# The first layer's down product and the short convolution's output product with tokens on partitions, in a two-layer decoder trunk

## The chip, the cores and the metric

The kernel runs on one core of a Trainium2 chip. The metric is the device time of one execution in microseconds. Before the change three runs took 2530.51 to 2531.64 us, with a median of 2531.28 us.

## The reference

Input and output are 256 tokens of 2048 features in float32. Layer 0 has a Mamba-2 mixer, layer 1 a short gated convolution; a gated feed-forward with a convolution over tokens follows each. Cut to what matters here:

```python
def rms_norm(x, w):
    y = x * rsqrt(mean(x * x, axis=-1) + 1e-5)
    return y * w

def conv_ffn(u, w_up, conv_w, conv_b, w_down):        # w_up 2048 x 11264, w_down 5632 x 2048
    hu = causal_dwconv(u @ w_up, conv_w, conv_b)       # width 3, over tokens
    g, v = split(hu, 2, axis=-1)
    return (silu(g) * v) @ w_down

def short_conv_mixer(u, w_in, conv_w, w_out):          # w_in 2048 x 6144, w_out 2048 x 2048
    bg, cg, h = split(u @ w_in, 3, axis=-1)
    return (bg * causal_dwconv(cg * h, conv_w)) @ w_out

x = x + ssd_mixer(rms_norm(x, mix_norm_w[0]), ...)
x = x + conv_ffn(rms_norm(x, ffn_norm_w[0]), ...)      # layer 0
x = x + short_conv_mixer(rms_norm(x, mix_norm_w[1]), ...)
x = x + conv_ffn(rms_norm(x, ffn_norm_w[1]), ...)      # layer 1
return rms_norm(x, final_norm_w)
```

## The kernel before

Every product is taken as three products of a split operand: a float32 array is cast to a high part in a reduced float32 format (`fp32r`), and the low part is what is left. High by high, high by low and low by high are added up in PSUM; low by low is left out.

**Weights.** All weights are loaded in blocks of 256 rows by 512 columns (`KU` = 2 tiles of 128 rows, `COLS` = 512), 512 KB each, in the order of the list `plan`, into four buffers `raw` (`load_raw`, line 330). `recipes` says what is made of them. A plain unit is one block's high part `wh` (ScalarE, line 352) and low part `wl` (VectorE, line 353). The units sit in four buffers and are made up to three ahead of use; `weight_unit` hands out the next. The program is written in order, and a scheduler places each engine's instructions by a simulated timeline; matmuls that go through `follow` keep their written order on TensorE.

**Streaming form** (`stream`, `late_stream`; features on partitions). The weights are the stationary operand, 128 by 128, and the activations of all 256 tokens the moving one. An activation tile `hl` has the high parts of 256 tokens and then the low parts, so `wh` takes one matmul of 512 columns and `wl` one of 256 (line 466). A unit is 8 of each. The result of four feature tiles lies in two PSUM tiles of two banks. `late_stream` works the second pair of feature tiles one unit behind the first; its argument `settle` sets how many matmuls of `wh` go before those of `wl`. All of the residual `x` lies in eight tiles `xp` with features on partitions. `residual_stream` adds a product to them (lines 854 and 855), squares them for the norm (`Norm.add`) and splits the next operand (`split_pair`). `Norm.row` sums the squares over partitions by matmuls (`tok_sum`, line 236), takes the reciprocal root per token, and spreads it over partitions by two matmuls (`bcast_tok`, line 229). The factor is applied to the next product's result, so the next product need not wait for it.

**Token form** (`down_tok`, line 1034; tokens on partitions). The activations are stationary, 128 tokens by 128 features, and the weights move, 512 columns at a time (lines 1070 to 1072: high by `wh`, high by `wl`, low by `wh`). So a block against both halves of the tokens is 2 x 2 x 3 = 12 matmuls. The residual lies in two tiles `xtok` of 128 tokens by 2048 features, and PSUM results are added to it by `add_x` (line 1080). The output columns go in two halves of two column groups. In a half the pairs of row blocks are worked in the order of a tuple in `DOWN`: a plain number is a pair of blocks (one for each column group), worked by 24 matmuls; `~j` is pair `j` worked by seven products in place of eight (Strassen's scheme in Winograd's form over two token halves, two row tiles and two column groups), 21 matmuls. For these `token_sums` makes sums and differences of the activations, and `load_unit` makes sums and differences of two weight blocks that are held together: recipes `t12`, `raw`, `t34` and `b22` (lines 374 to 383, on VectorE with casts on ScalarE). After a half's last such pair their seven sums are put together and added (the entry `e`).

Before the change the token form is used in layer 1's down product alone. Layer 1's feed-forward begins with the turn of `xp` into `xtok` by 32 transposes (line 997). The feed-forwards work their 5632 hidden features in two parts (`FPARTS`): part 0 has 24 tiles of 128 rows, part 1 has 20; each part's up product is followed by its down product. Stages in order: Mamba mixer (to about 704 us), layer 0's up and down products in two parts, the short convolution's input and output products, and layer 1's feed-forward, which ends with the final norm on `xtok`.

PSUM has three tiles of two banks (`psm`, tag `main`) and two of one bank (`psa`, tag `aux`).

Of the kernel before, what the change touches and what calls it, by code (L numbers as in the profile page):

```python
# [16 lines left out]
P = 128  # L17
# [31 lines left out]
def trunk_kernel(ctx, tc, a, out):  # L49
# [174 lines left out]
    def bcast_tok(r, dg=None):  # L224

        dg = dg or diag_tok(r)
        ps = aux()
        for c in range(2):
            mm(ps[:, c * P : (c + 1) * P], ones, dg[:, c, :], start=True, stop=True)
        return ps[:, :T]  # L230
# [87 lines left out]
    planned_all(c_out, 0, NKD)  # L318
# [124 lines left out]
    def late_stream(c0, hls, kcs, evac, settle=None):  # L443
# [395 lines left out]
    def residual_stream(hls, kcs, norm, nhl, nname, put=stream, parts=ALL_COLS):  # L839
# [7 lines left out]
        for cg, lo, hi in parts:  # L847
# [14 lines left out]
            put(cg * COLS, hls[lo // 2 : hi // 2], kcs[lo:hi], evac)  # L862
# [37 lines left out]
    def token_sums(y):  # L900


        st = pair_tmp()
        h0, h1 = slice(0, P), slice(P, T)
        tt(out=st[:, 0, h0], in0=y[:, 0, h1], in1=y[:, 1, h1], op=ALU.add)
        tt(out=st[:, 0, h1], in0=st[:, 0, h0], in1=y[:, 0, h0], op=ALU.subtract)
        tt(out=st[:, 1, h0], in0=y[:, 0, h0], in1=y[:, 0, h1], op=ALU.subtract)
        tt(out=st[:, 1, h1], in0=y[:, 1, h0], in1=st[:, 0, h1], op=ALU.subtract)
        sh, sl = (xpool.tile([P, 2, T], F32R, tag="x", name=uid("x")) for _ in range(2))
        nc.scalar.copy(sh, st)  # L910
        tt(out=sl, in0=st, in1=sh.bitcast(F32), op=ALU.subtract)
        return [(q[:, n // 2, (n % 2) * P : (n % 2 + 1) * P]) for n in range(4) for q in (sh, sl)]

    def ffn_part(l, part, hls, r):
        lo, hi = FPARTS[part]
        res, sums = [], {}
        for ch in range(lo, hi, 4):
            gs = []

            def evac_g(p, pt, ch=ch):  # L920
                k0 = ch + 2 * p
                y = conv(scaled(pt, r), W_FF, f"fw{l}", NF, k0, f"fb{l}", "g", gpool)
                act(y, y, AF.Silu)
                gs.append(y)

            def evac_v(p, pt, ch=ch):
                k0 = DFF // P + ch + 2 * p
                y = conv(scaled(pt, r), W_FF, f"fw{l}", NF, k0, f"fb{l}")
                tt(out=y, in0=gs[p], in1=y, op=ALU.mult)
                h = new_hl(hlpool2 if len(res) < 4 else hlpool)  # L930
                split_pair(h, y)
                if l == 1 and ~len(res) in DOWN[part][0] + DOWN[part][1]:
                    sums[len(res)] = token_sums(y)
                res.append(h)

            settle = {(0, 0): (2, None), (1, 0): (1, 1), (1, 4): (1, None), (1, 24): (2, 1)}
            settle = settle.get((l, ch), (None, None))
            late_stream(ch * P, hls, range(NKD), evac_g, settle[0])
            late_stream(DFF + ch * P, hls, range(NKD), evac_v, settle[1])
        return res, sums  # L940

    xhl, nhl = nhl, []
    r = norm.row()
    norm = Norm()
    for part in range(2):
# [8 lines left out]
    xhl, nhl = nhl, []  # L954
    r = norm.row()
    norm = Norm()
    r2 = small.tile([P, T], F32, tag="r2", name="r2", bufs=1)
    tt(out=r2, in0=r, in1=r, op=ALU.mult)
    yhl = []
    settle = {(0, 1): 1, (0, 2): 1}  # L960
    for i in range(D // COLS):
        vs = [None, None]

        def evac_c(p, pt):
            s = pair_sum(pt)
            tt(out=s, in0=s, in1=rep2(r2), op=ALU.mult)
            vs[p] = s

        def evac_h(p, pt):
            s = pair_sum(pt)  # L970
            tt(out=s, in0=s, in1=vs[p], op=ALU.mult)
            vs[p] = conv(s, W_SC, "scw", NKD, 4 * i + 2 * p)

        def evac_b(p, pt):
            s = scaled(pt, r)
            tt(out=s, in0=s, in1=vs[p], op=ALU.mult)
            h = new_hl()
            split_pair(h, s)
            yhl.append(h)

        for n, ev in ((1, evac_c), (2, evac_h), (0, evac_b)):
            late_stream(n * D + i * COLS, xhl, range(NKD), ev, settle.get((i, n)))
    residual_stream(
        yhl, range(NKD), norm, nhl, lambda m: ("ffn", NKD + 2 * m), late_stream
    )


    xhl = nhl
    r = norm.row()
# [13 lines left out]
    ss = small.tile([P, 2, 4], F32, tag="ss", name=uid("ss"))  # L1003

    most = [None, None]

    def begin_mean(c):

        sst = small.tile([P, 1], F32, tag="sst", name=uid("sst"))
        nc.vector.tensor_reduce(out=sst, in_=ss[:, c, 0:3], op=ALU.add, axis=mybir.AxisListType.X)  # L1010
        most[c] = small.tile([P, 1], F32, tag="most", name=uid("most"))
        ts(out=most[c], in0=sst, scalar1=0.5 / D, scalar2=0.5 * EPS, op0=ALU.mult, op1=ALU.add)

    def finish(c):

        v = small.tile([P, 1], F32, tag="var1", name=uid("var1"))
        stt(out=v, in0=ss[:, c, 3:4], scalar=0.5 / D, in1=most[c], op0=ALU.mult, op1=ALU.add)
        r = rsqrt_half(v)
        for q in (0, 1, 3, 2):
            x = xtok[c][:, q * COLS : (q + 1) * COLS]  # L1020
            if q == 3:
                stt(out=x, in0=x, scalar=r[:, 0:1], in1=fin[:, 3 * COLS :], op0=ALU.mult, op1=ALU.mult)
            elif q == 0:
                ts(out=x, in0=x, scalar1=r, scalar2=None, op0=ALU.mult)
            else:
                act(x, x, AF.Copy, scale=r)
            (nc.sync if q in (0, 3) else nc.scalar).dma_start(
                out=out[0, c * P : (c + 1) * P, q * COLS : (q + 1) * COLS], in_=x
            )

# [3 lines left out]
    def down_tok(hid, sums, lo, halves, done):  # L1034
# [7 lines left out]

        for half, order in enumerate(halves):
            cgs = (2 * half, 2 * half + 1)
            m23, m15, m67 = main_pair(), main_pair(), main_pair()
            bank = {
                1: m15[:, 0, :], 5: m15[:, 1, :], 6: m67[:, 0, :], 7: m67[:, 1, :],
                2: m23[:, 0, :], 3: m23[:, 1, :], 4: aux(), 8: aux(),
            }
            tail = order is LAST and half == 1  # L1050
            work = []
            for at, j in enumerate(order):
# [4 lines left out]
                elif not (tail and at >= len(order) - 2):  # L1057
                    work += [("p", j, m) for m in (2, 4, 3, 8)]
# [24 lines left out]
            for i, (kind, j, m) in enumerate(work):  # L1083
                if kind == "p":
# [5 lines left out]
                    if tail and i == len(work) - 5:  # L1090
# [3 lines left out]
                        block_done_of(done, 0, cgs[1])  # L1094
                elif kind == "s":
                    if m in (5, 1, 7, 3):
# [7 lines left out]
                else:  # L1104
                    add_x(0, 0, bank[1])
                    u = [tmp.tile([P, 512], F32, tag="tp", name=uid("tp")) for _ in range(3)]
# [13 lines left out]
            for m, c, g in () if tail else ends:  # L1120
                block_done_of(done, c, cgs[g])
    def block_done_of(done, c, cg):
        if done is not None:
            done(c, cg)

    for part in range(2):
        lo, hi = FPARTS[part]
        hid, sums = ffn_part(1, part, xhl, r)
# [44 lines left out]
```

## Time and profile before

| | before |
|---|---|
| median of three runs | 2531.28 us |
| the profiled execution's own time | 2532.64 us |
| span of its trace | 2530.8 us |
| granted TensorE clock, mean | 0.998 |
| HBM read | 474.09 MB |
| streaming matmuls of the late stages, line 466 | 4544 and 4544 |
| weight blocks of the down products, loaded | 176 x 512 KB |
| weight blocks of the short convolution's output product | 32 x 512 KB |

PE is the matmul engine, PEld its weight loads, DVE is VectorE, ACT ScalarE, POOL GpSimd and SP the engine that issues the weight loads. The chain is followed back from the last instruction: at each step to what released it, or to the instruction before it on its engine. In rows of the timeline the first number is the start in us from the span's beginning, the second the duration; in brackets stands an idle time before it with what ended it. Matmuls overlap, so the pace is the distance between starts and not the duration. A row of the waits says who waited for whom: the time in total, how often, and the longest.

### The profile page before, as it was taken

To read this page: it belongs to the slowest core of one execution; us is meant where nothing else is said; L and a number is where in the kernel's file an instruction comes from. 1 tells how busy PE (TensorE), PEld (TensorE's weight loads), DVE (VectorE), ACT (ScalarE), POOL (GpSimd) and SP (SyncE) were. 2 spreads that over 40 slices of the span, in tenths; PEclk is the share of its full clock that TensorE was granted. 3 is DMA by queue.
4 is the path that set the end of the run, shared out by engine and by line. 5 is a ranking of instruction groups with operands and counts; after the bars stand their busy time and mean duration, and the time that the engine had idled before them with its cause. 6 is when DMAs were issued, how large, how long until landed. Compare 5 with 4: busy or idle time off the path is not lost.

```text
span 2530.8 us, 37056 instructions
## 1 busy us (share of the span) xinstructions
PE 2510.2 (99%) x14358; PEld 2187.7 (86%) x14358; DVE 1868.8 (74%) x2630; ACT 1383.3 (55%) x1801; POOL 1.1 (0%) x8
## 2 busy tenths in 40 slices
PE   9999999999999999999999999999999999999998
PEld 8888888888888888888888888888888887888887
DVE  7788875788777776557776666666677778778787
ACT  5676654566555554345554444444555555455554
POOL 0000000000000000000000000000000000000000
PEclk9999999999999999999999999999999999999999
DMA  7566655665666665566666666665666666666654
GB/s 235 173 190 198 188 179 187 198 176 173 200 183 191 189 189 190 191 191 190 189 189 190 191 185 191 191 192 188 178 186 190 191 188 195 199 189 189 190 196 161
DMA packets 255731, 478.67 MB, mean 189 GB/s; under 512 B 17667, under 2 KB 29123, under 8 KB 255427
## 3 DMA queue, kind: packets, MB, share of 16 engines
q1 hardware_dynamic: 254643, 474.13, 61.8%
q8 instruction: 112, 1.84, 0.3%
q10 hardware_dynamic: 912, 2.18, 0.2%
q14 instruction: 64, 0.52, 0.1%
HBM read 474.09 MB, written 2.16 MB: 188 GB/s over the span
## 4 chain that ended last, share of the span: by engine, by line
PE 94%; DVE 3%; DMA 2%; ACT 0%; issue 0%; SPq 0%; DVEq 0%; ACTq 0%
PE main L466 62%; PE main L429 16%; PE main L412 8%; PE main L1071 1%; PE main L1072 1%; PE main L1070 1%; DMA raw<-in_ffn_w_down_dram 1%; DVE wl L353 1%; PE aux L1071 1%; PE aux L1070 1%; PE aux L1072 1%; PE aux L797 1%; DVE wl L383 1%; DMA cbc<-cs_d 0%; PE aux L805 0%
## 5 line engine op out<-in xcount | busy, mean ns | idle before, releaser
L466 PE MATMUL main<-hl,wh 128*128 128x512 f32 x4544 | 1568.4, 391 | 0.0
L353 DVE TENSOR_TENSOR wl<-raw,wh 128x1024 fp32r<-128x1024 f32 (+1 forms) x868 | 1058.7, 1222 | 583.0 <-ACT wh L352 573.7
L352 ACT CAST wh<-raw 128x1024 fp32r<-128x1024 f32 (+1 forms) x868 | 910.7, 1050 | 945.7 <-PE main L466 614.7
L466 PE MATMUL main<-hl,wl 128*128 128x256 f32 x4544 | 1256.0, 280 | 0.0
L466 PEld LDWEIGHTS main<-hl,wh 128*128 128x128 f32 x4544 | 845.1, 187 | 180.8
L466 PEld LDWEIGHTS main<-hl,wl 128*128 128x128 f32 x4544 | 856.4, 189 | 6.2
L429 PE MATMUL main<-hl,wh 128*128 128x512 f32 x1728 | 542.4, 397 | 1.3 <-DVE tp L492 1.3
L412 PEld LDWEIGHTS main<-hl,wl 128*128 128x128 f32 x1792 | 332.1, 188 | 75.6 <-DVE wl L353 2.8
L412 PE MATMUL main<-hl,wl 128*128 128x256 f32 x1792 | 359.8, 281 | 1.6 <-DVE wl L353 1.6
L429 PEld LDWEIGHTS main<-hl,wh 128*128 128x128 f32 x1728 | 266.5, 189 | 7.8 <-issue 4.9
L484 ACT COPY tp<-main 128x512 f32<-128x512 f32 x150 | 87.2, 581 | 30.9 <-PE main L466 23.9
L486 DVE TENSOR_TENSOR tp<-main,tp 128x512 f32<-128x512 f32 x150 | 102.4, 683 | 1.4 <-ACT tp L484 1.4
L508 DVE SCALAR_TENSOR_TENSOR tp<-tp,prm,tp 128x255 f32<-128x255 f32 x208 | 88.5, 477 | 0.0
L495 DVE TENSOR_TENSOR tp<-tp,rrow 128x512 f32<-128x512 f32 x118 | 81.3, 689 | 2.5
L508 DVE SCALAR_TENSOR_TENSOR g<-tp,prm,g 128x254 f32<-128x254 f32 (+1 forms) x176 | 73.4, 478 | 1.2 <-ACT g L506 1.2
L1071 PE MATMUL main<-wl,hl 128*128 128x512 f32 x150 | 58.4, 390 | 0.0
L1072 PE MATMUL main<-wh,hl 128*128 128x512 f32 x150 | 58.4, 389 | 0.0
L1070 PE MATMUL main<-wh,hl 128*128 128x512 f32 x150 | 58.4, 389 | 0.0
L382 ACT CAST wh<-tp 128x512 fp32r<-128x512 f32 x52 | 30.3, 617 | 43.2 <-DVE tp L374 40.5
L1071 PE MATMUL aux<-wl,hl 128*128 128x512 f32 x137 | 53.3, 389 | 0.0
L1072 PE MATMUL aux<-wh,hl 128*128 128x512 f32 x137 | 53.3, 389 | 0.0
L1070 PE MATMUL aux<-wh,hl 128*128 128x512 f32 x137 | 53.3, 389 | 0.0
(177 smaller groups left out, 1440.7 us busy)
## 6 DMA issues: line engine op xcount, KB each, us to landing
raw<-in_ffn_w_up_dram SPq DMA_DIRECT2D x352, 512.0 KB, 3.7
raw<-in_ffn_w_down_dram SPq DMA_DIRECT2D x176, 512.0 KB, 4.2
raw<-in_ssd_w_in_dram SPq DMA_DIRECT2D x159, 512.0 KB, 4.7
raw<-in_sc_w_in_dram SPq DMA_DIRECT2D x96, 512.0 KB, 3.7
raw<-in_ssd_w_out_dram SPq DMA_DIRECT2D x64, 512.0 KB, 3.8
raw<-in_sc_w_out_dram SPq DMA_DIRECT2D x32, 512.0 KB, 3.6
cbc<-cs_d SPq DMA_DIRECT2D x32, 256.0 KB, 6.0
xt<-in_x_dram SPq DMA_DIRECT2D x8, 256.0 KB, 6.8
```

The source lines that it names most:

```text
L352: put(nc.scalar.copy(wh[:, ks, :], raw[:, ks, :]))
L353: put(tt(out=wl[:, ks, :], in0=raw[:, ks, :], in1=wh[:, ks, :].bitcast(F32), op=ALU.subtract,))
L412: put(mm(pts[t // 2][:, t % 2, 0:T], wl[:, k, t * P : (t + 1) * P], hls[i // 2][:, i % 2, 0:T], start=False, stop=(i == n - 1),))
L429: put(mm(o, wh[:, k, lw], hl, start=first, stop=False))
L466: follow(mm(pts[p][:, t % 2, cols], w[:, k, t * P : (t + 1) * P], hl[:, cols], start=(i == 0 and w is wh), stop=(i == n - 1 and w is wl),))
L484: nc.scalar.copy(pb, pt[:, :, T : 2 * T])
L486: tt(out=s, in0=pt[:, :, 0:T], in1=pb, op=ALU.add)
L495: tt(out=s, in0=s, in1=rep2(r), op=ALU.mult)
L508: stt(out=y[:, j, d:T], in0=s[:, j, 0 : T - d], scalar=pcol(wname, (width - 1 - d) * nk + k0 + j), in1=y[:, j, d:T], op0=ALU.mult, op1=ALU ...
L1070: follow(mm(bank[m], ah, wh[:, k, :], start=first, stop=False))
L1071: follow(mm(bank[m], ah, wl[:, k, :], start=False, stop=False))
L1072: follow(mm(bank[m], al, wh[:, k, :], start=False, stop=last))
```

## The change

Layer 0's down product (both parts) and the short convolution's output product are worked by `down_tok`. The residual is turned into `xtok` once, ahead of layer 0's feed-forward, and stays with tokens on partitions from there on. What the next product needs with features on partitions is turned back: eight groups `turn(m)` of four transposes into one PSUM bank, from which `split_pair` makes an operand tile. The first four groups are put into the second half of the down product (entries `t`), the other four between the first units of the next product (`then`). The sum of squares is taken per token by ScalarE's accumulator (`TokNorm.add`), so the sum over partitions goes; the spreading over partitions stays. In a half with turns the banks are given out in another way (`apart`), so that `aux` tiles are free for the transposes. The order of layer 1's part 0 changes too: `~6` and `~9` each stand one place later.

```diff
 DOWN = (
-    ((1, 2, ~0, 4, 5, ~3, 7, ~6, 8, ~9, 10, 11), (1, 2, ~0, 4, 5, ~3, 7, ~6, 8, ~9, 10, 11)),
+    ((1, 2, ~0, 4, 5, ~3, 7, 8, ~6, 10, ~9, 11), (1, 2, ~0, 4, 5, ~3, 7, 8, ~6, 10, ~9, 11)),
     ((1, 2, ~0, 4, 5, ~3, 7, ~6, 8, 9), (1, 2, ~0, 4, 5, ~3, 6, 7, 8, 9)),
 )
+DOWN_TURN = (DOWN[0], (DOWN[1][0], (1, 2, 4, 5, ~0, 6, 7, ~3, 8, 9)))
+SC_TURN = ((1, 2, 0, 4, ~3, 5, 6, 7), (1, 2, 0, 4, 5, ~3, 6, 7))
...
-            if l == 1:
-                planned_tok(a["ffn_w_down"][l], lo, DOWN[part])
-            else:
-                planned_all(a["ffn_w_down"][l], lo, hi)
+            planned_tok(a["ffn_w_down"][l], lo, (DOWN if l else DOWN_TURN)[part])
...
-    planned_all(c_out, 0, NKD)
+    planned_tok(c_out, 0, SC_TURN)
...
-    def late_stream(c0, hls, kcs, evac, settle=None):
+    def late_stream(c0, hls, kcs, evac, settle=None, then={}):
...
             if u:
                 half(1, u - KU)
+            for f in then.get(u // KU, ()):
+                f()
...
+    class TokNorm:
+        def add(self, c, cg):
+            junk = tmp.tile([P, 512], F32, tag="tp", name=uid("tp"))
+            x = xtok[c][:, cg * COLS : (cg + 1) * COLS]
+            act(junk, x, AF.Square, accum_out=self.ss[:, c, cg : cg + 1])
+
+        def turn(self, m):
+            ps = aux()
+            for j in range(2):
+                for c in range(2):
+                    k = 2 * m + j
+                    follow(nc.tensor.transpose(
+                        ps[:, j * T + c * P : j * T + (c + 1) * P],
+                        xtok[c][:, k * P : (k + 1) * P], ident,
+                    ))
+            h = new_hl()
+            split_pair(h, ps.rearrange("p (a b) -> p a b", b=T), *self.nname(m))
+            self.nhl[m] = h
...
+        def then(self, pend, *more):
+            return {
+                1: pend[:1], 2: [pend[1], self.chain], 3: pend[2:3], 4: pend[3:],
+                6: [self.row, *more],
+            }
...
+    def down_tok(hid, sums, lo, halves, done=None, turn=None):
+        pend = []
         for half, order in enumerate(halves):
             cgs = (2 * half, 2 * half + 1)
-            m23, m15, m67 = main_pair(), main_pair(), main_pair()
-            bank = {
-                1: m15[:, 0, :], 5: m15[:, 1, :], 6: m67[:, 0, :], 7: m67[:, 1, :],
-                2: m23[:, 0, :], 3: m23[:, 1, :], 4: aux(), 8: aux(),
-            }
+            apart = turn is not None and half == 1
+            m23 = main_pair()
+            bank = {2: m23[:, 0, :], 3: m23[:, 1, :]}
+            if apart:
+                m48 = main_pair()
+                bank[4], bank[8] = m48[:, 0, :], m48[:, 1, :]
+            else:
+                bank[4], bank[8] = aux(), aux()
+            def more_banks():        # called at the half's first pair by seven products
+                m15 = main_pair()
+                bank[1], bank[5] = m15[:, 0, :], m15[:, 1, :]
+                if apart:
+                    bank[6], bank[7] = aux(), aux()
+                else:
+                    m67 = main_pair()
+                    bank[6], bank[7] = m67[:, 0, :], m67[:, 1, :]
...
                 elif not (tail and at >= len(order) - 2):
-                    work += [("p", j, m) for m in (2, 4, 3, 8)]
+                    for m in (2, 4, 3, 8):
+                        work.append(("p", j, m))
+                        if apart and (at, m) in ((0, 8), (1, 4), (1, 8), (2, 8)):
+                            work.append(("t", None, None))
...
+                elif kind == "t":
+                    pend.pop(0)()
...
+            elif turn is not None:
+                ends = ((4, 1, 0), (2, 0, 0), (8, 1, 1), (3, 0, 1))
...
+            if turn is not None:
+                pend += [(lambda m=m: turn(m)) for m in range(4 * half, 4 * half + 4)]
+        return pend
...
-                if l == 1 and ~len(res) in DOWN[part][0] + DOWN[part][1]:
+                if ~len(res) in DOWN[part][0] + DOWN[part][1]:
                     sums[len(res)] = token_sums(y)
...
-            settle = {(0, 0): (2, None), (1, 0): (1, 1), (1, 4): (1, None), (1, 24): (2, 1)}
+            settle = {
+                (0, 0): (1, 1), (0, 4): (1, None), (0, 24): (2, 1),
+                (1, 0): (2, 1), (1, 4): (1, None), (1, 24): (2, 1),
+            }.get((l, ch), (None, None))
...
-        hid, _ = ffn_part(0, part, xhl, r)
-        last = part == 1
-        residual_stream(
-            hid, range(*FPARTS[part]), norm if last else None, nhl,
-            lambda m: ("mix", NKD + 2 * m), late_stream,
-        )
+        hid, sums = ffn_part(0, part, xhl, r)
+        lo = FPARTS[part][0]
+        if part == 0:
+            down_tok(hid, sums, lo, DOWN_TURN[part])
+            continue
+        norm = TokNorm(lambda m: ("mix", NKD + 2 * m))
+        pend = down_tok(hid, sums, lo, DOWN_TURN[part], norm.add, norm.turn)
...
-    residual_stream(
-        yhl, range(NKD), norm, nhl, lambda m: ("ffn", NKD + 2 * m), late_stream
-    )
+    norm = TokNorm(lambda m: ("ffn", NKD + 2 * m))
+    pend = down_tok(yhl, sums, 0, SC_TURN, norm.add, norm.turn)
```

More of the change, by code (lines that the diff above doesn't have):

```diff
@@ L228, in bcast_tok @@
         for c in range(2):
[L229 removed]
+            put(mm(ps[:, c * P : (c + 1) * P], ones, dg[:, c, :], start=True, stop=True))
         return ps[:, :T]
@@ L837, in ssd_gate, with residual_stream @@
         return hls
-    def residual_stream(hls, kcs, norm, nhl, nname, put=stream, parts=ALL_COLS):
+    def residual_stream(hls, kcs, norm, nhl, nname, parts=ALL_COLS):
         if norm is not None:
@@ L1014, in finish, with __init__, chain, row @@
[L1014 to L1028, printed above, removed]
-            )
+    class TokNorm:
+        def __init__(self, nname):
+            self.ss = small.tile([P, 2, 4], F32, tag="ss", name=uid("ss"))
+            self.nname = nname
+            self.nhl = [None] * (NKD // 2)
+            self.r = []
+        def add(self, c, cg):
[14 more added lines that the diff above has]
+            self.nhl[m] = h
+        def chain(self):
+            sst = small.tile([P, 2], F32, tag="sst2", name=uid("sst2"))
+            nc.vector.tensor_reduce(
+                out=sst, in_=self.ss, op=ALU.add, axis=mybir.AxisListType.X
+            )
+            self.dg = diag_tok(mean_rsqrt(sst, D))
+        def row(self):
+            rb = small.tile([P, T], F32, tag="rrow", name=uid("rrow"))
+            nc.scalar.copy(rb, bcast_tok(None, self.dg, follow))
+            self.r.append(rb)
+        def then(self, pend, *more):
[3 more added lines that the diff above has]
+            }
@@ new lines, in ffn_part, with evac_g, evac_v @@
+    def ffn_part(l, part, hls, r, then={}):
+        lo, hi = FPARTS[part]
+        res, sums = [], {}
+        for ch in range(lo, hi, 4):
+            gs = []
+            def evac_g(p, pt, ch=ch):
+                k0 = ch + 2 * p
+                y = conv(scaled(pt, r[0]), W_FF, f"fw{l}", NF, k0, f"fb{l}", "g", gpool)
+                act(y, y, AF.Silu)
+                gs.append(y)
+            def evac_v(p, pt, ch=ch):
+                k0 = DFF // P + ch + 2 * p
+                y = conv(scaled(pt, r[0]), W_FF, f"fw{l}", NF, k0, f"fb{l}")
+                tt(out=y, in0=gs[p], in1=y, op=ALU.mult)
+                h = new_hl(hlpool2 if len(res) < 4 else hlpool)
+                split_pair(h, y)
+                if ~len(res) in DOWN[part][0] + DOWN[part][1]:
+                    sums[len(res)] = token_sums(y)
+                res.append(h)
+            settle = {
+                (0, 0): (1, 1), (0, 4): (1, None), (0, 24): (2, 1),
+                (1, 0): (2, 1), (1, 4): (1, None), (1, 24): (2, 1),
+            }.get((l, ch), (None, None))
+            late_stream(ch * P, hls, range(NKD), evac_g, settle[0], then if ch == lo else {})
+            late_stream(DFF + ch * P, hls, range(NKD), evac_v, settle[1])
+        return res, sums
@@ new lines, in trunk_kernel, with square_row @@
+    xhl = nhl
+    r = [norm.row()]
+    for part in range(2):
+        hid, sums = ffn_part(0, part, xhl, r)
[5 more added lines that the diff above has]
+        pend = down_tok(hid, sums, lo, DOWN_TURN[part], norm.add, norm.turn)
+    xhl, r, r2 = norm.nhl, norm.r, []
+    def square_row():
+        r2.append(small.tile([P, T], F32, tag="r2", name="r2", bufs=1))
+        tt(out=r2[0], in0=r[0], in1=r[0], op=ALU.mult)
@@ new lines, in trunk_kernel, with evac_c, evac_h, evac_b @@
+    then = norm.then(pend, square_row)
+    yhl, sums = [], {}
+    settle = {(0, 1): 2, (0, 2): 1, (0, 0): 1}
+    for i in range(D // COLS):
+        vs = [None, None]
+        def evac_c(p, pt):
+            s = pair_sum(pt)
+            tt(out=s, in0=s, in1=rep2(r2[0]), op=ALU.mult)
+            vs[p] = s
+        def evac_h(p, pt):
+            s = pair_sum(pt)
+            tt(out=s, in0=s, in1=vs[p], op=ALU.mult)
+            vs[p] = conv(s, W_SC, "scw", NKD, 4 * i + 2 * p)
+        def evac_b(p, pt):
+            s = scaled(pt, r[0])
+            tt(out=s, in0=s, in1=vs[p], op=ALU.mult)
+            h = new_hl()
+            split_pair(h, s)
+            if ~len(yhl) in SC_TURN[0] + SC_TURN[1]:
+                sums[len(yhl)] = token_sums(s)
+            yhl.append(h)
+        for n, ev in ((1, evac_c), (2, evac_h), (0, evac_b)):
+            late_stream(
+                n * D + i * COLS, xhl, range(NKD), ev, settle.get((i, n)),
+                then if (i, n) == (0, 1) else {},
+            )
@@ new lines, in trunk_kernel, with begin_mean @@
+    norm = TokNorm(lambda m: ("ffn", NKD + 2 * m))
+    pend = down_tok(yhl, sums, 0, SC_TURN, norm.add, norm.turn)
+    xhl, r = norm.nhl, norm.r
+    then = norm.then(pend)
+    ss = small.tile([P, 2, 4], F32, tag="ss", name=uid("ss"))
+    most = [None, None]
+    def begin_mean(c):
+        sst = small.tile([P, 1], F32, tag="sst", name=uid("sst"))
+        nc.vector.tensor_reduce(out=sst, in_=ss[:, c, 0:3], op=ALU.add, axis=mybir.AxisListType.X)
+        most[c] = small.tile([P, 1], F32, tag="most", name=uid("most"))
+        ts(out=most[c], in0=sst, scalar1=0.5 / D, scalar2=0.5 * EPS, op0=ALU.mult, op1=ALU.add)
@@ new lines, in finish @@
+    def finish(c):
+        v = small.tile([P, 1], F32, tag="var1", name=uid("var1"))
+        stt(out=v, in0=ss[:, c, 3:4], scalar=0.5 / D, in1=most[c], op0=ALU.mult, op1=ALU.add)
+        r = rsqrt_half(v)
+        for q in (0, 1, 3, 2):
+            x = xtok[c][:, q * COLS : (q + 1) * COLS]
+            if q == 3:
+                stt(out=x, in0=x, scalar=r[:, 0:1], in1=fin[:, 3 * COLS :], op0=ALU.mult, op1=ALU.mult)
+            elif q == 0:
+                ts(out=x, in0=x, scalar1=r, scalar2=None, op0=ALU.mult)
+            else:
+                act(x, x, AF.Copy, scale=r)
+            (nc.sync if q in (0, 3) else nc.scalar).dma_start(
+                out=out[0, c * P : (c + 1) * P, q * COLS : (q + 1) * COLS], in_=x
+            )
@@ L1126, in trunk_kernel @@
     for part in range(2):
         lo, hi = FPARTS[part]
-        hid, sums = ffn_part(1, part, xhl, r)
+        hid, sums = ffn_part(1, part, xhl, r, {} if part else then)
         def block_done(c, cg):
```

99 lines of the change are left out of this document (21 added, 78 removed).

## The prediction

> **What bounds the kernel now.** I read the engine totals first, then the chain that ended last, then the stages one by one.
>
> ```profile
> PE 2510.2 (99%) x14358; PEld 2187.7 (86%) x14358; DVE 1868.8 (74%) x2630; ACT 1383.3 (55%) x1801; POOL 1.1 (0%) x8
> ...
> PE 94%; DVE 3%; DMA 2%; ACT 0%; issue 0%; SPq 0%; DVEq 0%; ACTq 0%
> ...
> 723.73 723.18 PE main L466 x4172
> ...
> 704.00:837.00 133.00, 133.00 (x772) 117.16 (x771) 98.32 (x141) 75.23 (x97) 0.00 (x0) 1.00 0.63 186
> 970.00:1103.00 133.00, 133.00 (x770) 117.26 (x769) 73.86 (x77) 54.02 (x56) 0.00 (x0) 1.00 0.60 190
> 1793.00:2064.00 271.00, 271.00 (x1577) 239.12 (x1576) 204.74 (x294) 156.27 (x205) 0.00 (x0) 1.00 0.64 187
> 2064.00:2194.00 130.00, 127.44 (x556) 103.56 (x555) 111.83 (x149) 67.94 (x90) 0.00 (x0) 1.00 0.61 194
> ```
>
> TensorE is 99% busy and carries 94% of the chain. The long chain piece has 4172 streaming matmuls in 723.18 us with nothing between them: 0.1733 us each. The window rows give us, then PE, PEld, DVE, ACT and POOL busy, the clock, DMA share and GB/s: layer 0's first up products, its first down product, layer 1's first up products, and layer 1's first down product, the token form that the change copies. Only there is PE not full (127.44 of 130), and there DVE is at 86%. The clock is 1.00 throughout. So time is the number of matmuls times their pace, plus PE's gaps; work on other engines is free while it feeds PE in time.
>
> **The streaming form that goes.** A weight block (256 by 512) costs 16 matmuls, 16 x 0.1733 = 2.774 us. Layer 0's down product has 48 and 40 blocks, 133.1 and 110.9 us; the short convolution's output product has 32, 88.8 us. The same long piece shows that these stages hold no gap.
>
> **The token form that comes.** A block against both token halves is 12 matmuls, all 512 wide, so a plain pair of blocks is 24; a pair by seven products is 21. Its pace comes from the last down product: first and last matmul, 465 in all.
>
> ```profile
> 2415.60 0.39 PE L1070 MATMUL main<-wh,hl 128*128 128x512 f32 x1
> ...
> 2521.23 0.39 PE L1072 MATMUL aux<-wh,hl 128*128 128x512 f32 x1
> ...
> 2427.20 0.39 PE L1070 MATMUL main<-wh,x 128*128 128x512 f32 x1
> 2427.71 0.50 PE L1071 MATMUL main<-wl,x 128*128 128x512 f32 x1
> ...
> 2453.46 0.39 PE L1070 MATMUL main<-wh,x 128*128 128x512 f32 x1
> 2453.69 0.39 PE L1071 MATMUL main<-wl,x 128*128 128x512 f32 x1
> ```
>
> That is 105.63 us for 464 steps; less one stall (0.51 - 0.23 = 0.28, and 0.1 on the next step: 0.39) it is 0.2268 us a matmul. The last two rows are a pair of seven products without a stall: a step of 0.23. Counts: part 0 has 16 plain pairs and 8 by seven, 552 matmuls; part 1 has 15 and 5, 465; the output product 14 and 2, 378. Layer 0 becomes 125.2 and 105.5 us and the output product 85.7. That alone saves 7.9 + 5.4 + 3.1 = 16.4 us: 6.2 because 12 wide matmuls (2.722 us) beat 16 mixed ones (2.774) in 120 blocks, 10.2 because 15 pairs leave out three.
>
> **What the seven products cost: stalls.** Such a pair needs four converted sets (differences, then a high and a low part) from two loads held together. PE stalls at its first low-part matmul when VectorE has not got there. Layer 1's first down product:
>
> ```profile
> 2064.14 0.39 PE L1070 MATMUL main<-wh,hl 128*128 128x512 f32 x1
> ...
> 2075.74 0.39 PE L1070 MATMUL main<-wh,x 128*128 128x512 f32 x1
> 2076.24 0.50 PE L1071 MATMUL main<-wl,x 128*128 128x512 f32 x1
> ...
> 2091.83 0.39 PE L1070 MATMUL main<-wh,x 128*128 128x512 f32 x1
> 2092.14 0.50 PE L1071 MATMUL main<-wl,x 128*128 128x512 f32 x1
> ...
> 2102.25 0.39 PE L1070 MATMUL main<-wh,x 128*128 128x512 f32 x1
> 2103.16 0.50 PE L1071 MATMUL main<-wl,x 128*128 128x512 f32 x1 [0.52 <-DVE wl L383]
> ...
> 2113.27 0.39 PE L1070 MATMUL main<-wh,x 128*128 128x512 f32 x1
> 2114.22 0.50 PE L1071 MATMUL main<-wl,x 128*128 128x512 f32 x1 [0.55 <-DVE wl L383]
> ...
> 2166.49 0.40 PE L1070 MATMUL main<-wh,x 128*128 128x512 f32 x1
> 2168.26 0.50 PE L1071 MATMUL main<-wl,x 128*128 128x512 f32 x1 [1.37 <-DVE wl L383]
> ...
> 2178.37 0.39 PE L1070 MATMUL main<-wh,x 128*128 128x512 f32 x1
> 2178.73 0.50 PE L1071 MATMUL main<-wl,x 128*128 128x512 f32 x1
> ...
> 2193.59 0.61 PE L466 MATMUL main<-hl,wh 128*128 128x512 f32 x2
> ...
> DVE tp L374 <- DMA raw<-in_ffn_w_down_dram: 13.7, 7, 2.9
> ```
>
> Each step over 0.227, with the 0.1 behind it, is a stall: 0.40, 0.20, 0.80 and 0.83 in the first half, 1.65 and 0.25 in the second, 4.1 us together; the stage lasts 129.45 us against 125.2. The last row says what is late: seven times VectorE waited for a weight load to land (13.7 us in all), because the load's buffer came free late. Sorted by what stands ahead: after two plain pairs (eight cases with the last down product's) 0.40, 0.20, 0.39 and five times nothing, mean 0.12; after one plain pair (five cases) 0.80, 0.83, 1.65, 0.25 and 0 (the row at 2453.46), mean 0.71. Two plain pairs give the loads 5.4 us more.
>
> The new order has, in each part 0, six pairs with two or more plain ones ahead and two with one; layer 0's part 1 has four and one; the output product two and none. With both part 0s that is 18 and 5: 18 x 0.12 + 5 x 0.71 = 5.8 us. Ends: 0, and 18 x 0.40 + 5 x 1.65 = 15.5. I take the means, since layer 0's stages repeat layer 1's, with the same loads and conversions. Layer 1's part 0 should go from 129.45 to about 127.5; its part 1 is not changed.
>
> **Turning back.** Sixteen turns of four transposes, in PE's fixed order. The trace has them, in the first up product of layer 1:
>
> ```profile
> L997 PE MATMUL aux<-ident,x 128*128 128x128 f32 x32 | 4.3, 272 | 0.0
> ...
> 1816.55 1.03 PE L997 MATMUL aux<-ident,x 128*128 128x128 f32 x8
> 1817.34 0.36 PE L466 MATMUL main<-hl,wl 128*128 128x256 f32 x1
> 1817.54 0.39 PE L466 MATMUL main<-hl,wh 128*128 128x512 f32 x1
> ...
> 1832.30 0.60 PE L997 MATMUL aux<-ident,x 128*128 128x128 f32 x4
> 1832.65 0.48 PE L466 MATMUL main<-hl,wh 128*128 128x512 f32 x1
> 1832.97 0.28 PE L466 MATMUL main<-hl,wl 128*128 128x256 f32 x1
> ```
>
> Between the neighbours eight add 0.99 - 0.12 = 0.87 us and four add 0.67 - 0.23 = 0.44: 0.11 each, 64 x 0.11 = 7.0 us. Ends: 64 x 0.099 (0.79 for eight) = 6.3, and the row's own 272 ns unoverlapped, 17.4; I take the measured insertion. [...]
>
> The turns are also a new wait: everything of PE's stream is queued behind them, and each needs VectorE's additions into its columns. The half boundary in layer 1 shows when these end:
>
> ```profile
> 2129.23 1.28 DVE L1080 TENSOR_TENSOR xtok<-main,xtok 128x512 f32<-128x512 f32 x2
> 2130.43 0.68 DVE L1080 TENSOR_TENSOR xtok<-aux,xtok 128x512 f32<-128x512 f32 x1
> ```
>
> The half ends near 2129.0 (276 matmuls and the first four stalls, 2.2 us, after 2064.14), so the last addition is done 2 us later; the first turn comes 24 matmuls, 5.4 us, into the next half. The second four turns stand from the second unit of the next stream on, each three units (8.3 us) before its result is used, with two scalings and two subtractions between. I charge 0; ends 0 and, if the first turn of both stages were late by one 0.68 us addition, 1.4.
>
> **The rest.** Two token sums over partitions go:
>
> ```profile
> 1803.03 0.50 PE L236 MATMUL aux<-ones,nacc 128*128 128x1 f32 x4
> 1803.40 0.37 PE L466 MATMUL main<-hl,wl 128*128 128x256 f32 x1
> 1803.60 0.40 PE L466 MATMUL main<-hl,wh 128*128 128x512 f32 x1
> ```
>
> Each added 0.57 - 0.12 = 0.45 us, so 0.9 is saved; the broadcast stays. The 32 transposes with their eight ScalarE copies, and the load of the final norm's row, move from layer 1's start to layer 0's, at the same price. VectorE gains the block sums in layer 0's up products; layer 1's row has them already, at 76% busy with PE full. It loses the residual additions and squares per feature and gains 12 additions a half, all inside the 86% above. SP issues as many loads, the paired ones in another order, which is what the stalls price; POOL gets nothing. The other settings of matmul order keep the 0.1733 pace.
>
> **Sum.** Stages touched now: 133.1 + 110.9 + 88.8 + 129.45 = 462.3 us. After: 1947 matmuls x 0.2268 = 441.6, stalls 5.8, turns 7.0, sums -0.9, 0.2 for slow steps at a stage's start: 453.7. Saved 8.6 us (0.34%). The profiled execution took 2532.64 us around a span of 2530.8; the median, 2531.28, is 1.4 under it. 2531.3 - 8.6 = 2522.7.
>
> **Rivals.**
> - *Starved pairs, slower.* If the moved pairs stalled like the worst one (1.65) everywhere, 23 x 1.65 = 38.0 instead of 5.8 gives 2554.9. It breaks even at a mean of 0.63 us a pair and passes +0.2% at 0.86. For it: DVE at 86%, the 13.7 us of load waits. Against it: the mean of the 13 pairs now is 0.35, and most move farther apart. 7%.
> - *Spacing does not help.* Pairs with two ahead at 0.40, with one at 1.65: 15.5 us of stalls, 2532.4, no change. 12%.
> - *Transposes at their own duration.* 17.4 us instead of 7.0: 2533.1, no change. The rows above speak against it. 3%.
> - *Spacing cures all.* No stalls: 2516.9. The five cases without any speak for it, the first pair of a stage (0.40, 0.39) against. 14%.
>
> **Numbers.** The forecast has 64%, with 2519 to 2527 for its own range. Within 0.2% (5.1 us, about what a measurement here can tell) come the second and third rivals, 15%; slower the first, 7%; faster the forecast and the last, 78%. The range goes from the cure, with turns at their low end (2516.2), up to 2530, which leaves out the first rival, the third and part of the second.
>
> **What would show it.** Matmuls L466 fall by 2 x 960 = 1920 and token matmuls grow from 1017 to 2412. Layer 0's down stages should last about 127.5 and 109 us with the four turns in the second, the output product about 88; layer 1's part 0 about 127.5. Turns should show as four transposes adding 0.44 us, without an idle time before them. Steps over 0.3 us at a pair's first low part are the stalls; those after one plain pair should be the long ones. I am wrong if transposes carry idle time released by VectorE, if the up products of layer 0 gain gaps, or if stalls average above 0.6.

## The result and the profile after

The changed kernel is slower: 2543.85 us median of four runs (2541.33 to 2546.84), against 2530.9 before; the ratio is 1.0054, 95% interval 1.0036 to 1.0071. The forecast was 2522.7 us. The profiled execution took 2542.26 us, with a span of 2540.5. In the experiments e1, f1 and f4 one run each took 8868 to 11791 us where the others took some 2530; the medians and ratios below leave it out.

The lines that answer to those of before are the engine totals, the chain's shares, and from the waits the two in which PE waits longest (who for whom: us in total, times, longest):

```profile
PE 2512.7 (99%) x13889; PEld 2162.8 (85%) x13889; DVE 1948.5 (77%) x2800; ACT 1417.2 (56%) x1891; POOL 1.1 (0%) x8
...
PE 90%; DVE 5%; DMA 3%; issue 1%; ACT 1%; SPq 0%; DVEq 0%; ACTq 0%
...
PE aux L1022 <- DVE xtok L1032: 8.8, 2, 4.6
PE main L1023 <- DVE wl L352: 2.3, 8, 0.4
```

TensorE issues fewer matmuls, as counted, and its share of the chain fell from 94 to 90%: VectorE and loads came in. Two new kinds of wait are there. Twice a matmul into an `aux` bank waited over four microseconds for an addition to `xtok`; eight times the matmul with a plain unit's low part waited up to 0.4 us. The timeline of PE has the first long one, at the boundary between the halves of layer 0's part 0, and the two part 0s begin and end so:

```profile
973.03 0.39 PE L1022 MATMUL main<-wh,hl 128*128 128x512 f32 x1
...
1031.84 0.39 PE L1022 MATMUL main<-wh,hl 128*128 128x512 f32 x1
1032.59 0.50 PE L1023 MATMUL main<-wl,hl 128*128 128x512 f32 x1 [0.36 <-DVE wl L352]
...
1039.11 0.39 PE L1024 MATMUL main<-wh,hl 128*128 128x512 f32 x1
1044.09 0.79 PE L1022 MATMUL aux<-wh,hl 128*128 128x512 f32 x1 [4.60 <-DVE xtok L1032]
1044.68 0.63 PE L1023 MATMUL aux<-wl,hl 128*128 128x512 f32 x1
1045.11 0.63 PE L1024 MATMUL aux<-wh,hl 128*128 128x512 f32 x1
...
1108.93 0.39 PE L466 MATMUL main<-hl,wh 128*128 128x512 f32 x1
...
2066.90 0.39 PE L1022 MATMUL main<-wh,hl 128*128 128x512 f32 x1
...
2201.23 0.39 PE L466 MATMUL main<-hl,wh 128*128 128x512 f32 x1
```

From 1039.11 to 1044.09 is 4.98 us where 0.23 would do. Then the steps are 0.43 us instead of 0.23. Windows of that stretch show the clock (the columns are those of the windows before):

```profile
1031.00:1039.00 8.00, 7.63 (x34) 5.99 (x33) 7.67 (x9) 3.69 (x5) 0.00 (x0) 1.00 0.79 245
1039.00:1044.00 5.00, 0.50 (x3) 0.06 (x1) 5.00 (x9) 1.05 (x1) 0.00 (x0) 0.78 0.69 235
1044.00:1048.00 4.00, 3.91 (x9) 3.13 (x10) 2.69 (x6) 0.90 (x2) 0.00 (x0) 0.50 0.39 127
1048.00:1052.00 4.00, 4.00 (x17) 3.18 (x17) 1.30 (x3) 1.29 (x2) 0.00 (x0) 0.93 0.02 4
```

While PE waits, VectorE is busy all 5 us: it is the bound there. Behind the wait the granted clock is 0.50 for some 4 us. Together the boundary costs 4.75 + 0.36 + 9 x 0.2, about 7 us; the one in layer 1 (4.37) about 6. So the part 0s last 135.9 and 134.3 us (1108.93 - 973.03, 2201.23 - 2066.90) instead of the forecast 127.5. These two are 15 of the 18 us between the forecast span and the measured one.

Why VectorE is late stands in its own timeline between the last pair by seven and the boundary:

```profile
1028.92 0.68 DVE L382 TENSOR_TENSOR wl<-raw,wh 128x512 fp32r<-128x512 f32 x1
1029.53 1.88 DVE L1032 TENSOR_TENSOR xtok<-main,xtok 128x512 f32<-128x512 f32 x3
1031.32 3.49 DVE L352 TENSOR_TENSOR wl<-raw,wh 128x1024 fp32r<-128x1024 f32 x3
...
1041.62 1.22 DVE L352 TENSOR_TENSOR wl<-raw,wh 128x1024 fp32r<-128x1024 f32 x1
1042.75 0.69 DVE L373 TENSOR_TENSOR tp<-raw,raw 128x512 f32<-128x512 f32 x1
1043.35 1.28 DVE L1032 TENSOR_TENSOR xtok<-aux,xtok 128x512 f32<-128x512 f32 x2
```

After the last low part of the seven products VectorE makes three additions in a row (1.88 us) before the next plain unit's low part, which PE wants at 1032.07: the 0.52 us wait of 1032.59. The additions that free the `aux` banks come last, at 1043.35, behind the combination and behind weights of the next half; PE had ended the half at 1039.3.

Two edits of the diff are suspects, which the experiments test. The sequence of the combination (entry `e`) is new: both additions of bank 5 stand ahead of the copy, so three come together. And the order of part 0 is new: with `~9` one place later, one plain pair (5.4 us of PE) is left behind the last combination where there were two.

### The profile page after: what moved, and what is told of

It is laid out like the page before. It is cut to its first block, busy times and chain, and to the rows that moved or that the text cites. A ratio compares the mean times of both kernels' runs of the same rounds, so it can differ in the third digit from the quotient of the medians.

```text
span 2540.5 us, 36386 instructions
## 1 busy us (share of the span) xinstructions
PE 2512.7 (99%) x13889; PEld 2162.8 (85%) x13889; DVE 1948.5 (77%) x2800; ACT 1417.2 (56%) x1891; POOL 1.1 (0%) x8
## 4 chain that ended last, share of the span: by engine, by line
PE 90%; DVE 5%; DMA 3%; issue 1%; ACT 1%; SPq 0%; DVEq 0%; ACTq 0%
PE main L466 49%; PE main L428 16%; PE main L411 8%; PE main L1023 3%; PE main L1024 3%; PE main L1022 3%; DMA raw<-in_ffn_w_down_dram 2%; DVE wl L352 2%; PE aux L1022 2%; PE aux L1024 2%; PE aux L1023 2%; DVE wl L382 1%; DVE xtok L1032 1%; PE aux L799 1%; DMA raw<-in_ssd_w_in_dram 1%
## 5 line engine op out<-in xcount | busy, mean ns | idle before, releaser
L466 PE MATMUL main<-hl,wh 128*128 128x512 f32 x3584 | 1230.9, 392 | 0.0
L466 PE MATMUL main<-hl,wl 128*128 128x256 f32 x3584 | 972.7, 280 | 0.0
L466 PEld LDWEIGHTS main<-hl,wh 128*128 128x128 f32 x3584 | 661.4, 187 | 137.3
L466 PEld LDWEIGHTS main<-hl,wl 128*128 128x128 f32 x3584 | 673.3, 189 | 12.1
L428 PE MATMUL main<-hl,wh 128*128 128x512 f32 x1728 | 542.5, 397 | 1.3 <-DVE tp L494 1.3
L411 PEld LDWEIGHTS main<-hl,wl 128*128 128x128 f32 x1792 | 331.9, 188 | 76.0 <-DVE wl L352 3.3
L411 PE MATMUL main<-hl,wl 128*128 128x256 f32 x1792 | 359.9, 281 | 1.7 <-DVE wl L352 1.7
L428 PEld LDWEIGHTS main<-hl,wh 128*128 128x128 f32 x1728 | 266.5, 189 | 7.7 <-issue 4.9
L1023 PE MATMUL main<-wl,hl 128*128 128x512 f32 x423 | 167.0, 395 | 2.5 <-DVE wl L352 2.3
L1022 PE MATMUL main<-wh,hl 128*128 128x512 f32 x423 | 167.0, 395 | 0.0
L1024 PE MATMUL main<-wh,hl 128*128 128x512 f32 x423 | 166.0, 392 | 0.0
L1022 PE MATMUL aux<-wh,hl 128*128 128x512 f32 x269 | 106.1, 394 | 8.8 <-DVE xtok L1032 8.8
L1024 PE MATMUL aux<-wh,hl 128*128 128x512 f32 x269 | 106.0, 394 | 0.0
L1023 PE MATMUL aux<-wl,hl 128*128 128x512 f32 x269 | 105.9, 394 | 0.0
L1023 PEld LDWEIGHTS main<-wl,hl 128*128 128x128 f32 x423 | 80.0, 189 | 23.5 <-DVE wl L352 6.7
L1022 PEld LDWEIGHTS main<-wh,hl 128*128 128x128 f32 x423 | 80.0, 189 | 17.1
L1024 PEld LDWEIGHTS main<-wh,hl 128*128 128x128 f32 x423 | 79.8, 189 | 17.3
```

The costliest lines, as they stand in the source:

```text
L411: put(mm(pts[t // 2][:, t % 2, 0:T], wl[:, k, t * P : (t + 1) * P], hls[i // 2][:, i % 2, 0:T], start=False, stop=(i == n - 1),))
L428: put(mm(o, wh[:, k, lw], hl, start=first, stop=False))
L466: follow(mm(pts[p][:, t % 2, cols], w[:, k, t * P : (t + 1) * P], hl[:, cols], start=(i == 0 and w is wh), stop=(i == n - 1 and w is wl),))
L1022: follow(mm(bank[m], ah, wh[:, k, :], start=first, stop=False))
L1023: follow(mm(bank[m], ah, wl[:, k, :], start=False, stop=False))
L1024: follow(mm(bank[m], al, wh[:, k, :], start=False, stop=last))
```

## Experiments

The stage ahead of every edit ended anywhere from 700.2 to 705.6 us in the profiles, with edits and without; so I compare the medians and ratios of the runs, and lengths of stages. "Excess" of a stage is its length less 0.2268 us a matmul.

**Undoing the two edits, one by one and together; and the order alone on the kernel before.**

```diff
# e1 (changed kernel), e4: order of both part 0s
-    ((1, 2, ~0, 4, 5, ~3, 7, 8, ~6, 10, ~9, 11), (1, 2, ~0, 4, 5, ~3, 7, 8, ~6, 10, ~9, 11)),
+    ((1, 2, ~0, 4, 5, ~3, 7, ~6, 8, ~9, 10, 11), (1, 2, ~0, 4, 5, ~3, 7, ~6, 8, ~9, 10, 11)),
# e2: the reverse, in the kernel before
# e3 (changed kernel), e4: sequence of the combination
                     add_x(0, 0, bank[1])
-                    add_x(0, 1, bank[5])
-                    add_x(1, 1, bank[5])
...
                     add_x(0, 1, u[1])
+                    add_x(0, 1, bank[5])
                     add_x(1, 0, u[2])
                     add_x(1, 1, u[2])
+                    add_x(1, 1, bank[5])
```

> The changed kernel with part 0 of both layers back in the old order (~6 and ~9 one place earlier each, so two plain pairs stand behind the last pair by seven). Theory 'order': with one plain pair behind it, the last combination (its additions on VectorE) falls on the half's end and PE waits for an aux bank, 4.75 and 4.37 us, then runs at half clock. Then both waits go, with their slow clock (13 us), and the stalls at first low parts of the old order come back (some 2 us a part): about 2534 us. Rival 'banks': the new allotment of PSUM banks and the new order of the combination make the wait whatever the order: the waits stay and the time is 2543 or more.

> The kernel before with only layer 1's part 0 in the new order; nothing else is changed. Theory 'order': the wait of 4 to 5 us at the boundary of the halves and some 2 us of slow clock appear here too, while the stalls at first low parts fall from 4.3 to about 1.5: 3 to 4 us slower, about 2534. Rival 'banks': no wait at the boundary, the stalls fall: 2 to 3 us faster, about 2528.

> The changed kernel with the seven sums put together in the old sequence (the two additions of bank 5 at their old places instead of ahead of the copy). If the new sequence puts additions ahead of a plain pair's low part on VectorE, the stalls of 0.3 to 0.5 us behind each combination (ten halves) go: 3 to 4 us faster than the changed kernel, about 2540. Rival: those stalls come from the late loads; nothing changes, 2543 to 2545. Either way the boundary waits in both part 0s stay.

> The changed kernel with both undone: old order in both part 0s and old sequence of the combination. What is left of the change is the token form, the pairs by seven in the moved products, the turns and the new allotment of banks. If both theories hold: about 2530, faster than 2531 by what the working on record would give with the old order's stalls (462.3 before; after 441.6 + 4.3 + 4.3 + 1.6 + 7.0 - 0.9 = 457.9, so 4 us saved: 2527). Rival 'banks': 2543 or more.

| | median us | ratio to before (95%) | layer 0 part 0 | layer 1 part 0 | layer 1 part 1 |
|---|---|---|---|---|---|
| before | 2529.72 | 1 | - | 129.45 | 105.6 |
| changed | 2543.85 | 1.0054 (1.0036 to 1.0071) | 135.90 | 134.33 | 107.54 |
| e1 old order | 2532.32 | 1.0009 (1.0000 to 1.0019) | 127.99 | 128.62 | 108.02 |
| e2 before, new order | 2534.42 | 1.0020 (1.0011 to 1.0029) | - | 132.77 | 105.83 |
| e3 old combination | 2536.2 | 1.0029 (1.0017 to 1.0041) | 130.55 | 130.10 | 107.37 |
| e4 both old | 2525.13 | 0.9983 (0.9974 to 0.9992) | 127.27 | 127.58 | 106.56 |

(Before is the median of the 28 runs beside the four experiments, against which their ratios are taken; the changed kernel's ratio is to its own.) Theory "order" held in e1: both boundary waits are gone, and "banks" is out, for the new allotment of banks was still there. e2 shows the same from the other side: the kernel before, with nothing but the order changed, waits at the boundary of layer 1's part 0 and slows down behind it:

```profile
2130.75 0.39 PE L1072 MATMUL main<-wh,hl 128*128 128x512 f32 x1
2133.07 0.50 PE L1070 MATMUL aux<-wh,hl 128*128 128x512 f32 x1 [1.93 <-DVE xtok L1080]
2133.40 0.43 PE L1071 MATMUL aux<-wl,hl 128*128 128x512 f32 x1
2133.63 0.63 PE L1072 MATMUL aux<-wh,hl 128*128 128x512 f32 x1
```

But that wait is 2.1 us, not the 4.4 to 4.8 of the changed kernel. The other half of the expectation failed: the stalls inside the pairs by seven of that stage came to 3.7 us, not 1.5, where they were 4.1 before. So the gain that the new order was made for does not show in this profile. e3 gave more than the 3 to 4 us I expected, 6 to 8: the eight short waits went, and the boundary waits shrank to 2.05 us as well; behind each part 0 a new wait of 1.16 us stands at the start of the next stage. In its VectorE timeline one addition, not three, stands ahead of the weights, and the first `aux` bank is read 10.5 us after it (1037.86 - 1027.38) instead of 13.8 (1043.35 - 1029.53). Of the 3.3 us between them the two extra additions are only 1.2; one more low part and one difference of weights, which the scheduler now placed ahead of that read, make 1.7, and VectorE idled 0.3:

```profile
1027.38 0.68 DVE L1032 TENSOR_TENSOR xtok<-main,xtok 128x512 f32<-128x512 f32 x1
1027.98 2.34 DVE L352 TENSOR_TENSOR wl<-raw,wh 128x1024 fp32r<-128x1024 f32 x2
...
1037.86 0.68 DVE L1032 TENSOR_TENSOR xtok<-aux,xtok 128x512 f32<-128x512 f32 x1
```

With both undone (e4) no wait of PE for an addition is left; what PE still waits for in the token stages is three times a low part, 0.8 us in all:

```profile
PE main L1023 <- DVE wl L382: 0.8, 3, 0.3
```

e4 is faster than the kernel before, by 4.6 us in the medians (2.0 to 6.6 by the interval). Its stages from layer 0's first up product to the last matmul take 6.5 us less than before (1811.2 against 1817.6).

**The two edits without anything else.** g1 is the kernel before with the new combination alone, g2 with combination and order.

> The kernel before with only the sequence of the combination changed to the new one (both additions of bank 5 ahead of the copy), in layer 1's down product; old order. If three additions in a row ahead of a plain pair's low part are the cost, stalls of 0.3 to 0.5 us appear behind the combination in four halves, and no wait at a boundary, since two plain pairs stand behind it: 1.5 to 3 us slower than before. If the new sequence is only harmful together with the new banks or the turns: no change.

> The kernel before with the new order in part 0 and the new combination, layer 1 only: no moved product, no turn, no new allotment of banks. If these two edits are the whole loss, layer 1's part 0 takes some 134 us with a wait of 4 us or more at its boundary (before 129.45; the changed kernel 134.3) and its part 1 about 107.5 (before 105.6): 6 to 8 us slower than before. If the banks' allotment has a share in the long wait, the wait stays near the 2.09 us that the new order alone gave, and the time at 4 to 5 us slower.

g1: 2530.48 us, ratio 1.0008 (0.9999 to 1.0017); against 2528.89 for the runs beside it that is 1.6 us, not clear of zero. The waits behind the combination are there, four times 0.33 to 0.52 us. Part 0 is still no longer than before (129.28 us against 129.45), for its pairs by seven stalled 1.5 us less (2.6 against 4.1); part 1 grew by 0.9. One of the four:

```profile
2116.89 0.39 PE L1070 MATMUL main<-wh,hl 128*128 128x512 f32 x1
2117.62 0.50 PE L1071 MATMUL main<-wl,hl 128*128 128x512 f32 x1 [0.34 <-DVE wl L353]
```

g2: 2538.58 us, ratio 1.0043 (1.0026 to 1.0060): 9.7 us, more than the 6 to 8 expected. Layer 1's part 0 took 136.2 us and its boundary wait is back at the full size:

```profile
2131.32 0.79 PE L1070 MATMUL aux<-wh,hl 128*128 128x512 f32 x1 [4.19 <-DVE xtok L1080]
```

So the two edits, in layer 1 alone and with no moved product, turn or new bank allotment, cost 9.7 us. In the changed kernel, where they stand in layer 0 too, undoing both saved 18.7 (e4 against it). Both delays fall on the same queue: PE waits 2.1 us at the boundary with the order alone, not at all with the combination alone (e1, g1), and over 4 with both.

**What the order really decides.** f1 brings `~0` forward, f3 moves only `~9` back, f4 only `~6`; each on e4.

```diff
-  (1, 2, ~0, 4, 5, ~3, 7, ~6, 8, ~9, 10, 11)
+  (1, ~0, 2, 4, ~3, 5, 7, ~6, 8, ~9, 10, 11)    # f1
+  (1, 2, ~0, 4, 5, ~3, 7, ~6, 8, 10, ~9, 11)    # f3
+  (1, 2, ~0, 4, 5, ~3, 7, 8, ~6, ~9, 10, 11)    # f4
```

> Both undone as before, and both part 0s with the pairs by seven after 1, 2, 2 and 1 plain pairs and two plain pairs behind the last: (1, ~0, 2, 4, ~3, 5, 7, ~6, 8, ~9, 10, 11). If plain pairs ahead decide the stalls at first low parts, moving ~0 forward gives one more pair two ahead at the price of ~0 with one: 0 to 1 us against the kernel with both undone (2525.1), and no wait at the half boundary. If ~0 so early finds VectorE still busy with the up product's last results, it stalls over 1 us in each half: 2 to 5 us slower.

> Both undone, but ~9 one place later in both part 0s (two plain pairs ahead, one behind; ~6 at its old place). If what lies behind the last pair decides, the wait for an aux bank at the half boundary comes back at some 2 us with up to 1.7 of slow clock, and one of about 1 us at the stage's end, in each part 0: 4 to 7 us slower than 2525.1. If what lies ahead decides, it is 0 to 2 us faster.

> Both undone, but ~6 one place later in both part 0s, so that ~9 follows at once and two plain pairs stay behind. If what lies behind decides the boundary, there is none of that wait; ~9 with no plain pair ahead stalls at its first low part by more than the one-ahead mean, 1.5 to 4 us in each of four halves: 5 to 15 us slower than 2525.1. If spacing ahead does not matter, 2525.

f3: 2536.05 us, ratio 1.0023 (1.0014 to 1.0032), some 11 us slower than e4, where 4 to 7 were expected. The boundary waits came back, and with them waits at the start of the next stage, for a bank pair of the half before (four and two in the profile's waits):

```profile
PE aux L1022 <- DVE xtok L1032: 5.2, 4, 2.5
PE main L466 <- DVE xtok L1032: 1.9, 2, 1.0
```

f4: 2526.35 us, ratio 0.9985 (0.9976 to 0.9994), as fast as e4. `~9` with no plain pair ahead should have stalled by 1.5 us or more, by the view of my prediction. In the first half of layer 0's part 0 it begins at 1020.64 and loses 0.18 us once; the longer delay just ahead, 0.31 us, falls on the last of the seven products of `~6`, which has two plain pairs ahead of it. The three other halves are alike (at most 0.31 us at `~6`, 0.10 to 0.17 at `~9`, each before the 0.1 on the step behind it):

```profile
1020.07 0.50 PE L1023 MATMUL main<-wl,x 128*128 128x512 f32 x1 [0.15 <-DVE wl L382]
...
1020.64 0.39 PE L1022 MATMUL main<-wh,x 128*128 128x512 f32 x1
...
1022.41 0.50 PE L1023 MATMUL main<-wl,hl 128*128 128x512 f32 x1
```

So here the distance ahead of a pair does little, and the distance behind the last pair decides. f1: 2533.50 us, ratio 1.0013 (1.0004 to 1.0022), some 8 us slower than e4, more than the 2 to 5 of its rival. At the start of a stage the distance ahead does count. With one plain pair before it, `~0` meets VectorE still at the up product's last results, and PE waits twice:

```profile
981.98 0.50 PE L1023 MATMUL main<-wl,x 128*128 128x512 f32 x1 [0.49 <-DVE wl L382]
...
985.11 0.50 PE L1023 MATMUL aux<-wl,hl 128*128 128x512 f32 x1 [2.16 <-DVE wl L382]
```

Both part 0s have it; their excess went from 2.1 and 2.4 us to 4.7 and 6.4.

**What the moved pairs by seven are worth.** On e4:

```diff
-DOWN_TURN = (DOWN[0], (DOWN[1][0], (1, 2, 4, 5, ~0, 6, 7, ~3, 8, 9)))
-SC_TURN = ((1, 2, 0, 4, ~3, 5, 6, 7), (1, 2, 0, 4, 5, ~3, 6, 7))
+DOWN_TURN = ((tuple(range(12)),) * 2, (tuple(range(10)),) * 2)
+SC_TURN = (tuple(range(8)),) * 2
```

> Both undone, and the moved products (layer 0's down product, the output product) without pairs by seven: plain pairs only, block sums left out. 15 pairs give back 45 matmuls, 45 x 0.2268 = 10.2 us, and their stalls go (2.1 + 2.1 + 0.5 us of excess in these stages, of which about 3 belong to the pairs). If the pairs are worth their price: 7 us slower than with both undone, about 2532. Rival: the extra conversions also slow what lies around them and the pairs bring nothing: 2525 or less.

f2: 2535.85 us, ratio 1.0023 (1.0014 to 1.0032). The three moved stages take 131.88, 111.86 and 89.06 us, in e4 127.27, 109.05 and 87.70: the pairs save 8.8 of the 10.2 us that their 45 matmuls are worth. The medians differ by 10.7. Without the pairs the change is no gain at all: f2 is 6 us slower than the kernel before. By the working on record the turns' 7.0 us eat the 6.2 that the token form alone saves, which explains an even result; where the rest comes from is open.

## Why the prediction was wrong

*Pace, counts, turns: right.* Matmuls were 1920 fewer in the streaming form, and the two moved stages whose order was not at issue last 109.26 and 88.63 us in the changed kernel where 109 and 88 were forecast. In e4 the four stages last 127.27, 109.05, 87.70 and 127.58 us, close to the forecast 127.5, 109, 88 and 127.5. For the part 0s that is in part luck: 127.5 was meant for the new order, and e4 has the old one, for which the working gives 129.5 (125.2 + 4.3). A turn in the token form adds 0.36 + 0.09 = 0.45 us and does not wait (0.44 forecast):

```profile
1390.00 0.60 PE L936 MATMUL aux<-ident,xtok 128*128 128x128 f32 x4
1390.36 0.48 PE L1022 MATMUL main<-wh,hl 128*128 128x512 f32 x1
1390.68 0.40 PE L1023 MATMUL main<-wl,hl 128*128 128x512 f32 x1
```

A transpose's duration (272 ns in this trace, the mean of the 64 in the turns) is again not its price (0.45 / 4 = 0.11 us).

*The steps that failed.* First, VectorE "gains 12 additions a half, all inside the 86% above". The number of additions was right, their places were not looked at: the diff moves two of them ahead of work that PE waits for, and I gave that edit no term at all. By e4 against e1, and by e3 against the changed kernel, it costs about 7 us in the medians (4.8 in the stages of e1 and e4).

Second, the stalls "sorted by what stands ahead". The sorting fitted the 13 pairs of before, but I took a correlation for the cause; f4 contradicts it, and f3 shows the quantity that counts. The term was also mis-sized: the 23 pairs were charged 5.8 us and stalled 2.3. (The rows that the prediction shows as a pair's first low part belong to the second of its seven products; the first product's low part was in time.) The order change, given a gain of 2 us for layer 1, costs about 11 in the two layers (e1 against the changed kernel), and moving `~9` alone as much (f3 against e4).

Third, the half boundary: I read from the old order that the last addition is done 2 us after the half's end and used it for the turns alone. The trace of before says how little is spare: its two `aux` banks were read some 2 us ahead of their next use (the one of 2130.43 was free at 2131.11 and written again at 2133.16), and one plain pair, 5.4 us of PE, is what the new order takes from behind the last combination. I charged nothing for it; the runs showed waits of 4.75 and 4.37 us there, with some 4 us of slow clock. The row of before in which PE writes that `aux` bank again:

```profile
2133.16 0.39 PE L1070 MATMUL aux<-wh,hl 128*128 128x512 f32 x1
```

*The rivals.* None named this mechanism. The first, "starved pairs", put the loss at the pairs' first low parts, where layer 1's part 0 lost less than before (0.8 us against 4.1); its time, 2554.9, was not reached. (It passes +0.2% at 0.85 us a pair, not 0.86.) The forecast 2522.7 comes near to the kernel with both edits undone, 2525.13, in part by luck, since it counts on a gain from the new order that never came, while the stalls of the old order turned out smaller than before. Of the 8.6 us forecast, e4's stages show 6.5. 0.9 of the rest lies in layer 1's part 1, which I took as unchanged and which lasts 106.56 us instead of 105.63 with no long wait in it, only plain pairs some 0.15 us slower; why is open.

*Also open.* e4's layer 1 part 0 has the order and combination of before but an excess of 2.4 us against 4.3. What differs there is when the banks are taken and how the scheduler placed the rest; no run separates these.

## What to carry to other kernels

An order written for one engine also sets when the engine that empties its banks gets to its work (here `~9` one place later cost some 11 us, f3 against e4): count what a consumer must do between the last producer and the next use of each bank, not only what stands ahead of the producer. Where the consumer's engine is as busy as VectorE in these stages (86% in layer 1's part 0), moving two of its operations ahead of another needs a price of its own (here about 7 us), even if their number stays the same. And check a pattern read from a dozen cases against the other distance before it becomes a term of the sum.

## What the runs showed of the hardware

One short wait of PE cost nearly double: that of 2.05 us in e3 was followed by some 1.7 us lost to a granted clock of 0.50 (2127.20 to 2130.61 us). The 4.4 and 4.8 us waits of the changed kernel and the 4.3 of g2 were followed by 8 to 11 matmuls at 0.43 us, 1.9 times the usual 0.23, for some 4 us; in the changed kernel the granted clock was 0.50 there. Waits of 2 us did so in some cases and not in others: 2.09 (e2), 2.32 (f1) and one of 2.05 (e3) did; 2.33 (f1), 1.89 and 2.67 (f3) and the other 2.05 (e3) did not. So among these waits of 1.89 to 2.67 us length alone did not decide.

What looks like chance can be read off the traces. In those of the kernel before and of the changed one the moments at which the granted clock changes lie whole multiples of 3.4133 us apart: before, at 8.99, 12.41 and 2524.62 us (1 and 736 steps); in the changed kernel it is half (0.50) from 1041.77 to 1048.60 and from 2137.45 to 2140.86 us (2, 319 and 1 steps). Add up PE's waiting (distances between starts, less 0.23 us) in each step of such a grid, in all twelve traces without their first 20 and last few us. After the six steps at full clock that held 2.10 us or more, half clock followed: 2.10 (e3), 2.19 (e2), 2.27 (f1), 2.62 (g2), 2.43 and 2.98 (changed kernel). After none with less did it; the nearest were 2.00 and 1.98 (f3), 1.93 (f1) and 1.80 (e3). Of e3's two equal waits one lies whole inside a step and the other is cut by the grid at 1038.34 (the columns are those of the windows before; the clock is the 1.00 or 0.50 ahead of DMA share and GB/s):

```profile
2123.78:2127.20 3.42, 1.53 (x7) 0.96 (x6) 3.42 (x6) 1.05 (x1) 0.00 (x0) 1.00 0.66 215
2127.20:2130.61 3.41, 3.41 (x9) 2.65 (x9) 3.41 (x6) 0.62 (x1) 0.00 (x0) 0.50 0.59 178
...
1034.93:1038.34 3.41, 1.77 (x8) 1.12 (x6) 3.41 (x6) 1.65 (x2) 0.00 (x0) 1.00 0.81 269
1038.34:1041.75 3.41, 3.06 (x12) 2.18 (x12) 3.41 (x6) 0.17 (x1) 0.00 (x0) 1.00 0.53 174
```

The slow stretches behind these waits lasted one such step or two (3.41 us in e3, 6.83 and 3.41 us in the changed kernel), and in e3 a wait of 2.05 us, shorter than a step, had one behind it.
